# An 8192 x 8192 transpose on one core: one load issued in two parts with a meeting of the DMA engines behind it, and a branch hint in TensorE's loop

## The chip, the core and the metric

The kernel runs on one core of one Trainium2 chip. The metric is the device time of one execution in microseconds (us). Three runs of the kernel before took 1261.79, 1261.88 and 1262.31 us; their median, 1261.88 us, is the time before.

## The reference

```python
x = np.random.randn(8192, 8192).astype(np.float32)
def reference(x):
    return np.transpose(x)
```

The output is the transposed matrix in 32-bit floats. 268.44 MB are read from device memory (HBM) and 268.44 MB are written to it.

## The kernel before, in words

**Chunks.** The input is cut into T = 128 chunks of 128 rows by 4096 columns, 2 MB each (`chunks`, line 99): the left half of the columns first, from row 0 to row 8191 in 64 chunks, then the right half. Chunk t is loaded into one of NIN = 3 buffers, `ins[t % 3]`, with the 128 rows on the 128 partitions, so a load is 128 pieces of 16 KB (`load`, lines 101 to 105). The core's 16 DMA engines share each transfer: an engine takes 8 of the 128 rows. SyncE issues the first three loads; ScalarE issues all others and all stores, on its one queue, in the order of its program.

**TensorE.** `transposes(k)` (lines 112 to 123) waits until the semaphore of buffer k shows 18: 16 from the 16 DMA engines of the load, and one each from ScalarE and VectorE, which by then have emptied the PSUM halves of the chunk before. Then it makes 32 transposes of 128 x 128 blocks into the two PSUM tensors `pss[0]` and `pss[1]`. TensorE's program is a loop (lines 130 to 140) of 43 turns, three chunks in each but the first, which skips one by the `If` of line 135; the branch of line 140 closes it, and it is taken 42 times.

**Copies.** For each chunk, ScalarE copies PSUM half 0 and VectorE half 1 into the nine 2 MB regions of `regs` (line 236). A region gathers 512 output rows over W = 8 chunks; the eight groups of output rows are staggered, so that after the start one region is complete in each chunk. Before a region is filled anew, the copy waits for its earlier store (`fresh`, line 235).

**Stores and loads.** When a region is complete, `store` (lines 151 to 173) makes ScalarE wait for the copies (`s_cp`) and issue a store of 2 MB, 128 partitions by 4 output rows of up to 1024 elements. The first stores, of regions that start with fewer than eight chunks, are smaller, from 256 KB for chunk 0 up to 2 MB from chunk 7 on. At the end of chunk t's turn ScalarE waits until TensorE is done with the chunk (`s_pe`, line 250) and issues the load of chunk t + 3 (line 251). So ScalarE's program for one chunk is: copies with the store in between them or behind them, then the load of the chunk three further on. Each transfer has a semaphore that counts to 16: every DMA engine adds one, by a 4-byte packet, when its share is done. SyncE waits at the end for all stores (line 253).

Names that the prediction uses: `load`, `store`, `s_ld` (a load's semaphore), `s_st` (a store's), `regs`, and the loops of lines 133 to 140 (TensorE) and 179 to 251 (ScalarE and VectorE).

Of the kernel before, what the change touches and what calls it, by code (L numbers as in the profile page):

```python
# [24 lines left out]
def wide_dma(nc, eng, queue, out, in_):  # L25


    return eng.add_instruction(
        mybir.InstDMACopy(
            mode="Copy",  # L30
            name=nc.get_next_instruction_name(),
            engine=eng.engine,
            ins=[physical(in_)],
            outs=[physical(out)],
            queue=queue,
        )
    )
# [3 lines left out]
def kernel(  # L41
# [13 lines left out]
    nc = tc.nc  # L55
    P = 128
# [7 lines left out]
    NR = S // B  # L64
    NIN = 3
    NREG = 9
    CH = N // P
    J = S * P

    with tc.tile_critical():  # L70
        nc.alloc_sbuf_tensor("pad", [P, 32], dt)
        ident = nc.alloc_sbuf_tensor("ident", [P, P], dt).ap()
        ins = [nc.alloc_sbuf_tensor(f"in{k}", [P, J], dt).ap() for k in range(NIN)]
        SIZE = B * W * P
        regs = nc.alloc_sbuf_tensor("regs", [P, NREG * SIZE], dt).ap()
        NH = NR // 2
# [2 lines left out]
        s_id = nc.alloc_semaphore("s_id")  # L79
        s_ld = [nc.alloc_semaphore(f"s_ld{k}") for k in range(NIN)]  # L80
        s_st = [nc.alloc_semaphore(f"s_st{k}") for k in range(NREG)]
        s_pe = nc.alloc_semaphore("s_pe")
        s_cp = [nc.alloc_semaphore("s_cpa"), nc.alloc_semaphore("s_cpv")]

# [3 lines left out]
            out=ident,  # L88
            in_=ident,
# [8 lines left out]

        chunks = [(s, c) for s in range(M // J) for c in range(CH)]

        def load(t):
            s, c = chunks[t]
            (nc.sync if t < NIN else nc.scalar).dma_start(
                out=ins[t % NIN], in_=x[c * P:(c + 1) * P, s * J:(s + 1) * J]
            ).then_inc(s_ld[t % NIN], 16)

# [3 lines left out]
        def transposes(k):  # L112
            nc.tensor.sem_inc(s_ld[k], -18).wait_op(s_ld[k], 18, "sem-ge")  # L113
            for q in range(NR):
                e, g = divmod(q, NH)
                for b in range(B):
                    tr = nc.tensor.transpose(  # L117
                        pss[e][:, (g * B + b) * P:(g * B + b + 1) * P],
                        ins[k][:, q * B * P + b:(q + 1) * B * P - B + b + 1:B],
                        ident,  # L120
                    )
                if q % 2:
                    tr.then_inc(s_pe, 1)

        T = len(chunks)
# [4 lines left out]
        turn = nc.alloc_registers("turn", engines=pe)  # L130
        nc.regs_mov(turn, 0)
        nc.br("turns", engines=pe)
        with nc.body("turns", valid_engines=pe):
            now = nc.snap(turn, min_val=0, max_val=T // NIN)
            with nc.tensor.If(now > 0):
                transposes(NIN - 1)
            for k in range(NIN - 1):
                transposes(k)
            nc.regs_alu(turn, turn, 1, op=mybir.AluOpType.add)
            nc.tensor.br_lt(turn, T // NIN + 1, on_true="turns", on_false="done")  # L140
        nc.switch_bb("done")

        for t in range(NIN):
            load(t)

        copied = [0, 0]
        free = list(range(NREG))
        stored = [0] * NREG
        window = {}

        def store(q, e, count):
            t0, r, parts = window.pop(q)
            nc.scalar.wait_ge(s_cp[e], count)
            base = 0
            pieces = []
            for s, a, z in parts:
                rows = (z - a) * P
                j0 = s * J + q * B * P
                dst = out[j0:j0 + B * P, a * P:a * P + rows]
                dst = dst.rearrange("(q b) i -> q b i", q=P)  # L160
                src = regs[:, r * SIZE + base:r * SIZE + base + B * rows]
                base += B * rows
                pieces.append((rows, dst, src))
            for rows, dst, src in sorted(pieces, key=lambda v: -v[0]):
                if any(stored):
                    st = wide_dma(nc, nc.scalar, "qActDynamicHW", dst, src)
                else:
                    st = nc.scalar.dma_start(
                        out=dst, in_=src.rearrange("q (b i) -> q b i", b=B)
                    )  # L170
                st.then_inc(s_st[r], 16)
                stored[r] += 1
            free.append(r)

        def closes(w, t):
            t0, r, parts = w
            return t + 1 == t0 + sum(z - a for _, a, z in parts)

        for t, (s, c) in enumerate(chunks):
            for e in range(2):  # L180
                eng = (nc.scalar, nc.vector)[e]
                go = s_ld[(t + 1) % NIN]

                place = []
                fresh = {}
                for q in range(e * NH, (e + 1) * NH):
                    if q not in window:

                        span = (q - c) % W + 1
                        r = free.pop(0)
                        parts = [(s, c, min(c + span, CH))]
                        if c + span > CH and t + span < T:
                            parts.append((s + 1, 0, c + span - CH))
                        window[q] = (t, r, parts)
                        if stored[r]:
                            fresh[q - e * NH] = (s_st[r], 16 * stored[r])
                    t0, r, parts = window[q]
                    k = [p[0] for p in parts].index(s)  # L200
                    base = r * SIZE + B * P * sum(z - a for _, a, z in parts[:k])
                    _, a, z = parts[k]
                    place.append((base + (c - a) * P, (z - a) * P))

                runs = []
                for g in range(NH):
                    if runs:
                        u = runs[-1]
                        gap = place[g][0] - place[g - 1][0]
                        if place[g][1] == place[u[0]][1] and abs(gap) < 2 ** 15 and (  # L210
                            len(u) == 1 or gap == place[u[1]][0] - place[u[0]][0]
                        ):
                            u.append(g)
                            continue
                    runs.append([g])
                done = [g for g in range(NH) if closes(window[e * NH + g], t)]
                runs.sort(key=lambda u: any(g in fresh for g in u) - any(g in done for g in u))
                seen = t * NH + e * NH // 2
                for u in runs:
                    off, dist = place[u[0]]  # L220
                    gap = place[u[-1]][0] - place[u[-2]][0] if len(u) > 1 else 0
                    dims = [list(regs.ap[0]), [gap, len(u)], [dist, B], [1, P]]
                    o = bass.AP(regs.tensor, regs.offset + off, dims)
                    i = pss[e][:, u[0] * B * P:(u[-1] + 1) * B * P]
                    i = i.rearrange("p (l b i) -> p l b i", b=B, i=P)
                    last = u[-1]
                    if u is runs[-2:][0] and any(g in fresh for g in runs[-1]):
                        last = max(last, runs[-1][-1])
                    need = t * NH + (e * NH + last) // 2 + 1
                    if need > seen:  # L230
                        eng.wait_ge(s_pe, need)
                        seen = need
                    for g in u:
                        if g in fresh:
                            eng.wait_ge(*fresh[g])
                    cp = nc.scalar.copy(out=o, in_=i) if e == 0 else nc.vector.tensor_copy(out=o, in_=i)  # L236
                    ends = [e * NH + g for g in u if g in done]
                    if ends:
                        cp.then_inc(s_cp[e], 1)
                        copied[e] += 1  # L240
                    if u is runs[-1]:
                        if ends:
                            eng.wait_ge(s_cp[e], copied[e])
                            eng.sem_inc(go, 1)
                        else:
                            cp.then_inc(go, 1)
                    for q in ends:
                        store(q, e, copied[e])
            if t + NIN < T:
                nc.scalar.wait_ge(s_pe, (t + 1) * NR // 2)  # L250
                load(t + NIN)
        for r in range(NREG):
            nc.sync.wait_ge(s_st[r], 16 * stored[r])
# [30 lines left out]
```

## Time and profile before

| | |
|---|---|
| median of three runs | 1261.88 us |
| the profiled execution's own time | 1261.55 us |
| its span, first to last instruction | 1259.8 us |
| TensorE busy | 740.1 us, 4096 matrix instructions |
| VectorE busy | 302.6 us, 250 copies |
| ScalarE busy | 256.4 us, 256 copies |
| issues by ScalarE: loads | 125, 2048 KB each, median 22.5 us from issue to landing |
| issues by ScalarE: stores | 142; 114 of 2048 KB, median 18.4 us to landing |
| bytes moved | 536.95 MB, mean 426 GB/s |

The profile is of one execution. Its page gives the busy time of each engine, the span in 40 slices, the DMA queues (q1 is SyncE's, q10 is ScalarE's, q8 and q14 carry instructions that the engines fetch), and groups of instructions with what ended the idle time before them. The trace behind it answers for any stretch of the span: the timeline of an engine, the busy time and the DMA rate, and the number of DMA packets that start in a stretch, by size. In the loads and the 2 MB stores the only packets under 512 B are the 4-byte ones with which a DMA engine reports its share of a transfer as done. Their number in a narrow stretch therefore tells how many of the 16 engines finished a given transfer in it.

### The profile page before, as it was taken

Reading aid. Unit: us, or ns where it says so; the run is one execution under the profiler, and the core shown is the slowest. Engines: PE = TensorE matmul, PEld = TensorE weight load, DVE = VectorE, ACT = ScalarE, POOL = GpSimd, SP = SyncE. Lnnn points to the kernel's source line nnn. Section 1 sums busy time; section 2 is a strip of 40 time slices with the busy share of each in tenths; the row PEclk is TensorE's granted clock in tenths of the full one; section 3 lists DMA queues with packets and bytes.
Section 4 is the critical chain, followed back from the end, with each engine's and each line's share of the span. In section 5 each row is a group of like instructions: output and inputs, shape, how many; then the busy total and the mean of one; then the engine's idle time right before and its main releaser. Section 6 shows DMA issues by size and latency. Waiting matters only on the chain. (4 is left out here: it accounts for less than half of the span.)

```text
span 1259.8 us, 9405 instructions
## 1 busy us (share of the span) xinstructions
PE 740.1 (59%) x4096; PEld 719.5 (57%) x4096; DVE 302.6 (24%) x250; ACT 256.4 (20%) x257; POOL 0.7 (0%) x6
## 2 busy tenths in 40 slices
PE   5656656565566656565555656565566656565561
PEld 5556656565556655565555655565565656565551
DVE  2322222222222222222222222222222222222220
ACT  2212121121211211122211221221111211121120
POOL 0000000000000000000000000000000000000000
PEclk9886776768777777778687786868777786868776
DMA  9999999999999999999999999999999999999998
GB/s 385 427 427 429 429 427 431 428 430 430 428 431 428 430 432 428 430 430 429 430 424 426 431 429 429 430 429 431 429 430 431 429 430 431 428 431 429 430 431 355
DMA packets 39271, 536.95 MB, mean 426 GB/s; under 512 B 4320, under 2 KB 4832, under 8 KB 6240
## 3 DMA queue, kind: packets, MB, share of 16 engines
q10 hardware_dynamic: 38832, 530.60, 98.9%
q1 hardware_dynamic: 432, 6.29, 1.2%
q14 instruction: 6, 0.05, 0.0%
q8 instruction: 1, 0.02, 0.0%
HBM read 268.44 MB, written 268.44 MB: 426 GB/s over the span
## 5 line engine op out<-in xcount | busy, mean ns | idle before, releaser
L117 PE MATMUL ps<-ident,in 128*128 128x128 f32 x4096 | 740.1, 362 | 491.8 <-PEq L113 491.8
L117 PEld LDWEIGHTS ps<-ident,in 128*128 128x128 f32 x4096 | 719.5, 219 | 512.3 <-issue 512.3
L236 DVE COPY regs<-ps 128x512 f32<-128x512 f32 (+3 forms) x250 | 302.6, 1246 | 930.9 <-PE ps L117 903.0
L236 ACT COPY regs<-ps 128x512 f32<-128x512 f32 (+3 forms) x256 | 255.1, 1014 | 975.0 <-PE ps L117 756.7
L236 ACT ACT_TABLE_LOAD x1 | 1.3, 1283 | 1.0 <-SPq L70 1.0
L87 POOL TENSOR_SCALAR_AFFINE_SELECT ident<-ident 128x128 f32<-128x128 f32 x1 | 0.3, 294 | 0.2 <-POOL ident L85 0.2
L85 POOL MEMSET ident<- 128x128 f32 x1 | 0.2, 205 | 0.5 <-SPq L70 0.5
L268 POOL MEMSET const-bfloat16-1.0<- 128x1 bf16 x1 | 0.1, 102 | 0.0
L268 POOL MEMSET const-uint8-127<- 128x1 uint8 x1 | 0.1, 102 | 0.0
L268 POOL MEMSET const-float32-0.0<- 128x1 f32 x1 | 0.1, 99 | 0.2 <-issue 0.2
L268 POOL MEMSET const-float32-1.0<- 128x1 f32 x1 | 0.1, 99 | 0.0
## 6 DMA issues: line engine op xcount, KB each, us to landing
in<-in_x_dram ACTq DMA_DIRECT2D x125, 2048.0 KB, 22.5
out_dram<-regs ACTq DMA_DIRECT2D x114, 2048.0 KB, 18.4
out_dram<-regs ACTq DMA_DIRECT2D x4, 1792.0 KB, 15.1
in<-in_x_dram SPq DMA_DIRECT2D x3, 2048.0 KB, 11.7
out_dram<-regs ACTq DMA_DIRECT2D x4, 1536.0 KB, 15.8
out_dram<-regs ACTq DMA_DIRECT2D x4, 1280.0 KB, 15.8
out_dram<-regs ACTq DMA_DIRECT2D x4, 1024.0 KB, 17.1
out_dram<-regs ACTq DMA_DIRECT2D x4, 768.0 KB, 18.7
```

The source lines that it names most:

```text
L85: nc.gpsimd.memset(ident, 0.0).then_inc(s_id, 1)
L87: nc.gpsimd.affine_select(out=ident, in_=ident, compare_op=mybir.AluOpType.not_equal, fill=1.0, base=0, pattern=[[-1, P]], channel_multipl ...
L117: tr = nc.tensor.transpose(pss[e][:, (g * B + b) * P:(g * B + b + 1) * P], ins[k][:, q * B * P + b:(q + 1) * B * P - B + b + 1:B], ident,)
L236: cp = nc.scalar.copy(out=o, in_=i) if e == 0 else nc.vector.tensor_copy(out=o, in_=i)
L268: nc = _bacc.Bacc("TRN2", target_bir_lowering=False, num_devices=1)
```

## The change

1. The load of chunk 10 (`MEET + NIN - 1`, with `MEET = 8`) is issued as two transfers, rows 0 to 79 (`MOST = 80`, five rows for each DMA engine) and rows 80 to 127 (three rows for each). The first adds to a new semaphore, `s_most`; only the second adds to the buffer's `s_ld`.
2. In chunk 8's turn the store is not issued where its copy stands. It is held back until all copies of the turn are issued and ScalarE has seen 16 in `s_most`. The load of chunk 11 stands behind it, as before, and so do all later transfers. That load of chunk 10 is the last transfer issued ahead of the wait.
3. TensorE's loop gets one more instruction at its head in every turn, a branch prefetch hint (`mark_branch_hint_location`), tied to the branch that closes the loop.

```diff
+    MEET = 8
+    MOST = 80
...
+        s_most = nc.alloc_semaphore("s_most")
...
         def load(t):
             s, c = chunks[t]
-            (nc.sync if t < NIN else nc.scalar).dma_start(
-                out=ins[t % NIN], in_=x[c * P:(c + 1) * P, s * J:(s + 1) * J]
-            ).then_inc(s_ld[t % NIN], 16)
+            eng = nc.sync if t < NIN else nc.scalar
+            cuts = [0, MOST, P] if t == MEET + NIN - 1 else [0, P]
+            for a, z in zip(cuts, cuts[1:]):
+                eng.dma_start(
+                    out=ins[t % NIN][a:z], in_=x[c * P + a:c * P + z, s * J:(s + 1) * J]
+                ).then_inc(s_ld[t % NIN] if z == P else s_most, 16)
...
             now = nc.snap(turn, min_val=0, max_val=T // NIN)
+            hint = nc.tensor.mark_branch_hint_location()
             with nc.tensor.If(now > 0):
...
-            nc.tensor.br_lt(turn, T // NIN + 1, on_true="turns", on_false="done")
+            nc.tensor.br_lt(
+                turn, T // NIN + 1, on_true="turns", on_false="done"
+            ).branch_hint(hint)
...
+        held = []
...
                     for q in ends:
-                        store(q, e, copied[e])
+                        if t == MEET:
+                            held.append((q, e, copied[e]))
+                        else:
+                            store(q, e, copied[e])
+            if t == MEET:
+                nc.scalar.wait_ge(s_most, 16)
+                for q, e, count in held:
+                    store(q, e, count)
             if t + NIN < T:
                 nc.scalar.wait_ge(s_pe, (t + 1) * NR // 2)
                 load(t + NIN)
```

## The prediction

> **What bounds the kernel now.** I read the page first: the span in slices, then the groups with their idle time.
>
> ```profile
> span 1259.8 us, 9405 instructions
> ...
> DMA  9999999999999999999999999999999999999998
> GB/s 385 427 427 429 429 427 431 428 430 430 428 431 428 430 432 428 430 430 429 430 424 426 431 429 429 430 429 431 429 430 431 429 430 431 428 431 429 430 431 355
> ...
> L117 PE MATMUL ps<-ident,in 128*128 128x128 f32 x4096 | 740.1, 362 | 491.8 <-PEq L113 491.8
> ```
>
> The 16 DMA engines are busy throughout, at 424 to 432 GB/s in every slice but the first and the last. TensorE idles 491.8 us, always at line 113, where it waits for a load or for the copies. So the DMA engines are the bound. The question is which of the sixteen, and the windows of the trace answer it (columns: stretch and length, busy time and count of PE, PEld, DVE, ACT and POOL, then clock, DMA share, GB/s).
>
> ```profile
> 1100.00:1200.00 100.00, 61.08 (x332) 59.47 (x332) 23.86 (x20) 20.54 (x20) 0.00 (x0) 0.72 1.01 430
> ...
> 1254.20:1258.60 4.40, 0.00 (x0) 0.00 (x0) 0.00 (x0) 0.00 (x0) 0.00 (x0) 0.50 0.20 79
> ```
>
> In mid-run no engine pauses (share 1.01), and 430 / 16 = 26.9 GB/s per engine puts a 16 KB row at 0.61 us. In the last 4.4 us the share is 0.20: some engines still work while most have finished. The end is set by the engine that lags most.
>
> How large the lag is at load 10 can be counted. Three stretches, 78.9 to 80.1, 80.1 to 82.5 and 82.5 to 82.8 us; packets under 512 B are engines that report their share as done:
>
> ```profile
> DMA packets 45, 0.49 MB, mean 410 GB/s; under 512 B 15, under 2 KB 15, under 8 KB 15
> ...
> DMA packets 63, 1.03 MB, mean 430 GB/s; under 512 B 0, under 2 KB 0, under 8 KB 0
> ...
> DMA packets 8, 0.11 MB, mean 382 GB/s; under 512 B 1, under 2 KB 1, under 8 KB 1
> ```
>
> Fifteen engines finish load 10 within 1.2 us, one about 3 us later (82.6 against 79.5). The same for load 126, in 1211.85 to 1212.8, 1213.6 to 1214.2, 1214.2 to 1215 and 1215.8 to 1216.2 us (the stretches between these hold none):
>
> ```profile
> DMA packets 35, 0.39 MB, mean 414 GB/s; under 512 B 11, under 2 KB 11, under 8 KB 11
> ...
> DMA packets 17, 0.26 MB, mean 437 GB/s; under 512 B 1, under 2 KB 1, under 8 KB 1
> ...
> DMA packets 21, 0.31 MB, mean 389 GB/s; under 512 B 2, under 2 KB 2, under 8 KB 2
> ...
> DMA packets 13, 0.18 MB, mean 451 GB/s; under 512 B 2, under 2 KB 2, under 8 KB 2
> ```
>
> Eleven engines still go together, but five now lag, the last two by about 4 us behind the first. Measured from the first reporter, the late engine of load 10 went from 3.6 to 3.75 us behind to 3.95 to 4.35: it slipped 0.2 to 0.75 us in 116 chunks. The other of the last two was in the group of fifteen, so it went from at most 1.2 us to about 4.1: it slipped 2.75 us or more.
>
> **The change part by part.**
>
> *The meeting.* It removes no byte. An engine that is ahead will stand still until the late one has caught up, and that alone moves neither the late engine nor the end. Two things can move the end: whether the late engine itself runs dry, and how the sixteen slip against each other afterwards.
>
> ScalarE around the place, and TensorE's start on chunk 10 and after:
>
> ```profile
> 61.70 0.93 ACTq L103 DMA_DIRECT2D in<-in_x_dram  x1
> 65.36 0.59 ACT L236 COPY regs<-ps 128x512 f32<-128x512 f32 x1 [6.21 <-PE ps L117]
> 65.98 0.55 ACTq L28 DMA_DIRECT2D out_dram<-regs  x1
> ...
> 68.64 0.33 ACTq L103 DMA_DIRECT2D in<-in_x_dram  x1
> 77.82 1.01 ACT L236 COPY regs<-ps 128x1024 f32<-128x1024 f32 x1 [9.66 <-DMA out_dram<-regs]
> 78.86 0.55 ACTq L28 DMA_DIRECT2D out_dram<-regs  x1
> 79.45 1.01 ACT L236 COPY regs<-ps 128x1024 f32<-128x1024 f32 x1 [0.62 <-ACT regs L236]
> 79.47 0.94 ACTq L103 DMA_DIRECT2D in<-in_x_dram  x1
> ```
>
> ```profile
> 83.08 5.57 PE L117 MATMUL ps<-ident,in 128*128 128x128 f32 x32 [4.63 <-PEq L113]
> 92.80 5.57 PE L117 MATMUL ps<-ident,in 128*128 128x128 f32 x32 [4.15 <-PEq L113]
> ```
>
> Load 10 goes out at 61.70. Today store 8 (65.98) and load 11 (68.64) queue up behind it. With the change both wait for the late engine's first five rows. Its last row is reported at 82.6, so its fifth is at 82.6 - 3 x 0.61 = 80.8. From report to waiter takes 83.08 - 82.6 = 0.45 us (TensorE on chunk 10), so ScalarE issues store 8 at about 81.2. What an issue into idle engines costs, the trace shows once, at the start: SyncE issues at 0.94; the stretches are 0.94 to 1.95 and 1.95 to 2.35 us.
>
> ```profile
> 0.94 1.32 SPq L103 DMA_DIRECT2D in<-in_x_dram  x3
> ```
>
> ```profile
> DMA packets 0, 0.00 MB, mean 0 GB/s; under 512 B 0, under 2 KB 0, under 8 KB 0
> ...
> DMA packets 16, 0.26 MB, mean 655 GB/s; under 512 B 0, under 2 KB 0, under 8 KB 0
> ```
>
> That is 1.0 to 1.4 us, so data flow again at 82.2 to 82.6, just as the late engine ends its last three rows (82.6). It pauses 0 to 0.2 us; I take **+0.2**. The upper bound is ScalarE's first store, issued behind SyncE's loads: no packet of it by 14.8 us.
>
> ```profile
> 10.98 0.65 ACTq L168 DMA_DIRECT2D out_dram<-regs  x1
> ...
> q1 hardware_dynamic: 114, 1.61, 98.6%
> ```
>
> From 10.98 to 14.8 only q1 moved: 3.8 us, which would restart at 85.0 and cost 2.4 us. That store had other traffic ahead of it, so the lower row is nearer. [...]
>
> What queues behind the wait on ScalarE: store 8, load 11, then chunk 9's copies (now 77.82 and 79.45), its store and load 12. From 81.2: two issues of 0.55 and up to 0.94 us, the copy at about 82.7 to 83.7, store 9 at 83.8, the second copy to 85, load 12 by 86. Chunk 10's transposes wait for that copy: 85 instead of 83.08. TensorE's idle time covers it (4.15 us before chunk 11, whose load lands at about 92.8 in either case). Store 8 and load 11 keep the DMA engines busy, at 2.1 MB and 430 GB/s or 4.9 us each, to 82.4 + 2 x 4.9 = 92.2, and store 9 and load 12 are in the queue by then. So nothing runs dry a second time: **0**, and if store 9 came later than 92.2 its delay would be the cost.
>
> *The slip afterwards.* All sixteen start level with the late engine, so the end is now set by whichever slips most over the remaining 117 chunks. If the old slips repeat, that is the engine with about 3.2 instead of the late one with about 0.6: +2.6 (between 2.0 and 4.1 by the counts above). If the slips of the leaders came from running out of phase with the late engine, level engines would not repeat them: 0. If nothing slips at all, the late engine's own 0.6 is saved: -0.6. No row tells which. I take the middle of the first two, **+1.3**, and keep -0.6 and +2.6 for the range.
>
> *The split.* One more issue (0.33 to 0.94 us) on ScalarE at 62, hidden in the idle time before its copy at 65.36, and 16 more 4-byte packets: **0**; without that cover under 1 us once.
>
> *The hint.* One more TensorE instruction in 43 turns, beside 491.8 us of idle time: 0 on TensorE even at half a microsecond each (22 us). Its effect can only be in the fetches, which the DMA engines carry:
>
> ```profile
> q14 instruction: 6, 0.05, 0.0%
> q8 instruction: 1, 0.02, 0.0%
> ```
>
> One 16 KB packet on q8. The stretch 19 to 21 us holds it, and in it TensorE ends its first turn and branches back, at 15.48 + 4.11 = 19.6:
>
> ```profile
> q8 instruction: 1, 0.02, 2.9%
> ```
>
> ```profile
> 15.48 4.11 PE L117 MATMUL ps<-ident,in 128*128 128x128 f32 x32 [1.71 <-PEq L113]
> ```
>
> All 16 engines report load 2 in 17.3 to 17.9; fifteen report load 3 in 23.3 to 23.9 and one in 24.5 to 24.65:
>
> ```profile
> DMA packets 226, 0.11 MB, mean 179 GB/s; under 512 B 16, under 2 KB 226, under 8 KB 226
> ...
> DMA packets 52, 0.16 MB, mean 273 GB/s; under 512 B 15, under 2 KB 15, under 8 KB 51
> ...
> DMA packets 17, 0.07 MB, mean 437 GB/s; under 512 B 1, under 2 KB 1, under 8 KB 17
> ```
>
> So the fetch put about 1.0 us on one engine (0.6 to 1.35), and the late engine begins there. A hint in turn 0 runs at about 2 us, when load 0 has begun; the fetch would cost the same engine the same 1.0 under load 0. I take **0**; if it comes for free, -1.0.
>
> Sum: 1261.55 + 0.2 + 0 + 1.3 + 0 + 0 = 1263.05 us in the profiled execution's terms; the median of the runs stands 0.33 above that execution, so 1263.4.
>
> **The rivals.**
>
> *A: the engines ahead slip as before* (ends on the other side, slower). Mechanism: level engines meet the same fetches and collisions as before, and one slips 3.2 where the late one slips 0.6. Price: 0.2 + 2.6, that is 1264.7; with a pause of 2.4 it is 1266.9. It decides from a worst slip of 2.9 us on, where the sum passes 0.2%. For it: five engines did fall behind after load 10. Against: 11 of 16 didn't.
>
> *B: the hint fetches in every turn.* 42 packets of 16 KB on one engine, 0.61 to 1.0 us each: 26 to 42 us, 1288 to 1304. Against it: the kernel before takes the branch 42 times and q8 shows one packet, so the loop stays in the instruction memory. [...]
>
> *C: the fetch leaves the data's way and level engines hardly slip.* -1.0 - 0.6 + 0.2 gives 1260.5; if more of the late engine's 3.1 us at load 10 came from TensorE's fetches than the one recorded packet, another 1 to 2 us go, down to 1258.5. Against it: the one packet explains a third of the lag, and no other is recorded before load 10.
>
> *D: the meeting does not level the engines*, since restart is staggered or slips return at once: the old lag of 4 us with the pause, 1262.1.
>
> **How the numbers follow.** Forecast with D, 1261 to 1264.4: 0.43. A: 0.29. B: 0.07. C: 0.21, about half of it with further fetches. The predicted time is 1263.4. The range runs from 1259.8 (C without its far end) to 1266.9 (A with the longest pause); B and that far end of C stay out. A measurement of this kernel can tell about 0.2%, 2.5 us, from no change. Faster by more than that, below 1259.36, needs C's further fetches: 0.11. Slower by more, above 1264.4, is A and B: 0.36. Within: 0.53.
>
> **What would show it.** Store 8 issued at about 81.2 instead of 65.98; sixteen reports of load 11 within about 1 us; a dip of the DMA rate near 80 to 82.5 us only. Late in the run, reports of one load spread over 1 to 4 us: the slip. One q8 packet or none: B is wrong. My forecast is wrong if the last engine pauses over 1 us, if q8 shows tens of packets, or if the spread at the end is under 0.6 us.

## The result, and the profile after

The changed kernel takes 1269.3 us in the median of six runs (1268.34 to 1273.97), the kernel before 1262.24 us in six runs beside it (1261.79 to 1262.65). The ratio is 1.0063, with a 95% interval of 1.0047 to 1.0078: slower by 5.9 to 9.8 us. The profiled executions have spans of 1266.5 and 1259.8 us.

From the page of the changed kernel: the span, the DMA rate in 40 slices of 31.7 us, and the queues.

```profile
span 1266.5 us, 9450 instructions
...
GB/s 385 424 349 423 427 429 427 428 430 430 429 429 431 429 430 431 428 428 430 430 424 423 432 429 429 430 429 430 430 430 430 430 430 431 428 430 431 428 430 360
...
q10 hardware_dynamic: 38848, 530.60, 98.9%
q1 hardware_dynamic: 432, 6.29, 1.2%
q14 instruction: 6, 0.05, 0.0%
```

One slice stands out: 349 GB/s in the third, where the kernel before has 427. The bytes that are missing there are 78 / 429 x 31.7 = 5.8 us of full rate. And q8 has no packet in the span: the fetch at TensorE's first backward branch is gone.

Where the 6.7 us of the profiled executions arise can be read from TensorE's starts. They are the arrivals of loads 9, 10 and 11 on the last DMA engine; the kernel before has 72.92, 83.08 and 92.80.

```profile
70.86 5.56 PE L123 MATMUL ps<-ident,in 128*128 128x128 f32 x32 [3.73 <-PEq L119]
86.85 6.44 PE L123 MATMUL ps<-ident,in 128*128 128x128 f32 x32 [10.43 <-PEq L119]
96.64 6.63 PE L123 MATMUL ps<-ident,in 128*128 128x128 f32 x32 [3.35 <-PEq L119]
```

Chunk 9 starts 2.1 us earlier, chunk 10 3.8 us later. So between the two 5.8 us are lost. Chunk 11 is still 3.8 us late, the end 6.7: another 2.9 us are lost behind it. Most of them go soon: chunk 20 starts at 187.39 us instead of 181.04, 6.35 us late.

The trace also keeps the time at which each engine's report of a load lands, a little behind the start of the 4-byte packet that the windows count (below: "by the reports"). By these, the mean of the sixteen engines is 6.3 us later than before at load 10 and 6.9 at load 126. So the sixteen together lose only 0.6 us behind the meeting. The rest is one engine that falls behind the others again: the last report of load 10 lands 0.4 us behind the mean of its sixteen, that of load 20 2.8 and that of load 126 2.7.

ScalarE around the wait, and the windows of the stretch before and behind it (columns as in the prediction's windows, the last two are the DMA share and GB/s):

```profile
58.29 1.18 ACTq L109 DMA_DIRECT2D in<-in_x_dram  x2
...
81.77 0.55 ACTq L28 DMA_DIRECT2D out_dram<-regs  x1
82.35 0.60 ACTq L109 DMA_DIRECT2D in<-in_x_dram  x1
83.05 1.01 ACT L246 COPY regs<-ps 128x1024 f32<-128x1024 f32 x1 [16.35 <-issue]
```

```profile
65.00:75.00 10.00, 6.27 (x41) 6.11 (x40) 2.29 (x1) 1.44 (x1) 0.00 (x0) 0.84 1.01 424
75.00:80.00 5.00, 1.42 (x11) 1.23 (x9) 2.29 (x1) 0.00 (x0) 0.00 (x0) 0.84 1.04 239
80.00:85.00 5.00, 0.00 (x0) 0.00 (x0) 0.00 (x0) 1.33 (x2) 0.00 (x0) 0.50 1.02 157
```

Store 8 goes out at 81.77, near the 81.2 of the prediction. But no engine stands idle for it: the DMA share is 1.02 to 1.04 throughout. The rate has fallen to 239 GB/s from 75 us on, before anything waits, and to 157 GB/s in the second five microseconds. The engines are busy with the two parts of load 10, and their rows take some 1.3 us each in the mean, by the packets' own durations, where others take 0.61.

At the end the engines are apart again. Reports of one load in 1218.55 to 1219.25, 1220.5 to 1220.85, 1221.6 to 1221.7 and 1222.2 to 1222.9 us:

```profile
DMA packets 30, 0.34 MB, mean 492 GB/s; under 512 B 9, under 2 KB 9, under 8 KB 9
...
DMA packets 9, 0.10 MB, mean 281 GB/s; under 512 B 3, under 2 KB 3, under 8 KB 3
...
DMA packets 8, 0.10 MB, mean 983 GB/s; under 512 B 2, under 2 KB 2, under 8 KB 2
...
DMA packets 22, 0.33 MB, mean 468 GB/s; under 512 B 2, under 2 KB 2, under 8 KB 2
```

Nine engines go together, seven lag by 1.3 to over 3 us: as in the kernel before. At load 10 they had been level, but not by the meeting. The reports of store 7, ahead of the wait, show it: sixteen in 74.5 to 75.3 us with the change, against fifteen in 74.1 to 74.85 and one in 77.3 to 77.4 us in the kernel before.

```profile
DMA packets 36, 0.33 MB, mean 410 GB/s; under 512 B 16, under 2 KB 16, under 8 KB 16
```

```profile
DMA packets 35, 0.33 MB, mean 437 GB/s; under 512 B 15, under 2 KB 15, under 8 KB 15
...
DMA packets 4, 0.05 MB, mean 492 GB/s; under 512 B 1, under 2 KB 1, under 8 KB 1
```

The late engine is gone before the wait, and with the hint alone (next section) it is gone too. So it is the hint that levels the engines in the changed kernel.

### The profile page after: what moved, and what is told of

It reads as the page before. It is cut to its first block, busy times and chain, and to the rows that moved or that the text cites. A ratio compares the mean times of both kernels' runs of the same rounds, so it can differ in the third digit from the quotient of the medians.

```text
span 1266.5 us, 9450 instructions
## 1 busy us (share of the span) xinstructions
PE 740.2 (58%) x4096; PEld 719.6 (57%) x4096; DVE 302.6 (24%) x250; ACT 256.4 (20%) x257; POOL 0.7 (0%) x6
```

## The experiments

Each run's kernel was timed beside the kernel before; the differences below are to those runs. All are given in the median.

**One part of the change at a time.** First the hint alone: the diff of TensorE's loop is kept, the rest undone.

```diff
+            hint = nc.tensor.mark_branch_hint_location()
...
-            nc.tensor.br_lt(turn, T // NIN + 1, on_true="turns", on_false="done")
+            nc.tensor.br_lt(
+                turn, T // NIN + 1, on_true="turns", on_false="done"
+            ).branch_hint(hint)
```

> The hint alone: load 10 whole, no wait. In the changed kernel the last DMA engine reported store 7 at 76.0 us instead of 77.7, so the hint seems to take one or two instruction fetches (1 us each) off one engine early on. Theory S (slips come back whatever the start): the last engine is about 1.7 us earlier at 80 us, but other engines fall behind later and the spread at the end is again about 4 us: 1261.5 to 1262.3. Theory F (the others only slip because of the late engine): the spread at the end stays under 1.5 us and the time is 1259 to 1260. Theory H (the hint costs time): over 1262.5, with packets on q8 in every turn.

1263.07 us against 1261.61; ratio 1.0015 (1.0006 to 1.0024). Theory H's range, over 1262.5, has the number, but not for its reason: q8 has no packet in the span. Chunk 9 starts 2.1 us early, as in the changed kernel, so what the hint removes is real. It is lost again. A part goes in the window 83 to 132 us, first with the hint alone, then in the kernel before.

```profile
70.83 6.46 PE L120 MATMUL ps<-ident,in 128*128 128x128 f32 x32 [3.69 <-PEq L116]
```

```profile
83.00:132.00 49.00, 30.77 (x152) 29.96 (x151) 11.67 (x7) 10.12 (x10) 0.00 (x0) 0.67 1.01 424
```

```profile
83.00:132.00 49.00, 29.58 (x160) 28.77 (x160) 11.59 (x7) 10.13 (x10) 0.00 (x0) 0.71 1.01 429
```

With no late engine all sixteen together are slower, 424 instead of 429 GB/s, which is 0.6 us in this window. By the reports, the last engine is 2.3 us early at load 10 and 1.6 us late at load 126: in between the sixteen lose 2.7 us in the mean, and the last one falls 1.3 us further behind the mean.

Then the split alone: 80 and 48 rows, no wait, no hint.

```diff
+            cuts = [0, MOST, P] if t == MEET + NIN - 1 else [0, P]
+            for a, z in zip(cuts, cuts[1:]):
+                eng.dma_start(
+                    out=ins[t % NIN][a:z], in_=x[c * P + a:c * P + z, s * J:(s + 1) * J]
+                ).then_inc(s_ld[t % NIN] if z == P else s_most, 16)
```

> Load 10 in two parts of 80 and 48 rows, no wait and no hint. [...] Theory W (the wait is what costs): 1261.9 to 1262.3, no dip.

1269.26 us, 7.6 more, without the wait, and so far above theory W's range: 5.0 us are there at chunk 10 and 7.0 at the end of the profiled execution. The slice and the start of chunk 10 show the same loss as the changed kernel (348 GB/s in the third slice; 88.08 instead of 83.08):

```profile
GB/s 386 425 348 427 427 429 429 429 430 429 430 430 430 428 429 430 429 429 430 429 420 425 429 430 430 429 430 430 430 428 430 430 430 430 429 430 430 429 430 350
```

```profile
88.08 5.21 PE L123 MATMUL ps<-ident,in 128*128 128x128 f32 x32 [9.72 <-PEq L119]
```

So the loss in the slice belongs to the split, not to the wait.

**The wait without the dear split.** Load 10 is cut by columns, so both parts have all 128 rows.

```diff
-    MOST = 80
+    MOST = 2560
...
-            cuts = [0, MOST, P] if t == MEET + NIN - 1 else [0, P]
+            cuts = [0, MOST, J] if t == MEET + NIN - 1 else [0, J]
...
-                    out=ins[t % NIN][a:z], in_=x[c * P + a:c * P + z, s * J:(s + 1) * J]
+                    out=ins[t % NIN][:, a:z], in_=x[c * P:(c + 1) * P, s * J + a:s * J + z]
```

> The changed kernel, but load 10 is cut by columns: 2560 columns of all 128 rows first, then 1536 columns. Bytes per engine, wait and hint are the same as in the changed kernel; only the rows' fall on the partitions is that of a whole load. [...] Theory W: 1267 to 1269, as in the changed kernel.

> As the run with columns and the wait, but without the hint: this is the case of the prediction's sum (meeting of unequal engines, no dear split). [...] Theory F (level engines slip little): 1261.3 to 1262.2. Theory W: 1267 or more.

With the hint 1265.88 us, 4.3 more than before; without it 1267.94, 6.3 more. The dear split is gone, and still the run without the hint lies in theory W's range, and the one with it only 1.1 us below. So the wait itself costs far more than I had put down. In the run without the hint, ScalarE's issue, TensorE's start on chunk 11, and then the rate in slices:

```profile
80.65 0.55 ACTq L28 DMA_DIRECT2D out_dram<-regs  x1
```

```profile
94.18 5.57 PE L123 MATMUL ps<-ident,in 128*128 128x128 f32 x32 [3.74 <-PEq L119]
```

```profile
GB/s 384 426 375 422 421 425 425 426 430 428 431 430 431 429 430 430 428 430 430 429 421 423 429 430 430 430 430 431 429 429 429 430 430 429 430 431 430 430 429 359
```

Chunk 11 starts 1.4 us late (94.18 against 92.80), the end is 6.1 us late (span 1265.9): 4.7 us come after the meeting is long over. In the slices from 95 to 250 us the rate is 421 to 426 GB/s, where the kernel before has 427 to 431.

The first 1.4 us are no pause of the last engine. Its last report of load 10 falls at 82.12. Of the sixteen engines' first rows of store 8, fifteen start in the stretch 81.8 to 82.1 us, and the sixteenth starts in 82.1 to 82.15 us, together with that report:

```profile
DMA packets 16, 0.25 MB, mean 840 GB/s; under 512 B 0, under 2 KB 0, under 8 KB 1
...
DMA packets 2, 0.02 MB, mean 328 GB/s; under 512 B 1, under 2 KB 1, under 8 KB 1
```

What follows is slow although the engines are busy, 324 GB/s at a share of 1.02:

```profile
84.00:88.00 4.00, 3.28 (x16) 3.31 (x17) 0.00 (x0) 0.58 (x1) 0.00 (x0) 0.50 1.02 324
```

By the packets' own durations, the last rows of store 8, and then those of load 11, take up to about 1.2 us instead of 0.61. The run with the hint has the same: its engines are level ahead of the wait, none stands for more than 0.6 us between load 10 and store 8, and still the sixteen lose 2.1 us in the mean between loads 10 and 11, by the reports. So a part of the wait's cost lies in the two transfers behind it, and why they are slow is open. Of the 4.7 us further on, in the run without the hint, the sixteen lose 2.3 in the mean; the rest is one engine that falls behind anew, from 0.3 us behind the mean at load 11 to 2.8 at load 126.

Next the cover is made longer: 1024 columns first, 3072 behind them, so that each engine still has 3.7 us of work when the last one reports.

```diff
-    MOST = 2560
+    MOST = 1024
```

> The wait at chunk 8 with load 10 cut by columns, no hint, but 1024 columns first and 3072 behind them, so that each engine still has 3.7 us of work when the last one reports (before: 1.8 us, and 1267.9 us in the median). If the pause of the last engine, about 1.0 us, was part of the cost, it goes: 1266.5 to 1267.2. If the whole cost is the slipping behind the wait: 1267.6 to 1268.3.

1265.47 us, 3.5 us more than the kernel before, against 6.3 with 2560 columns: the gain is larger than either expectation had it. The reports of store 8 now spread over 85.76 to 87.11 us instead of 87.42 to 88.04: with a longer cover the engines ahead wait less and are levelled only in part. There was no pause to save. The run fits that levelling costs, but it doesn't show it: the wait also ends at another moment of the load.

**Why the split is dear.** Four loads cut into 80 and 48 rows; load 10 in halves; load 10 in 32, 64 and 32 rows. No wait, no hint.

```diff
-            cuts = [0, MOST, P] if t == MEET + NIN - 1 else [0, P]
+            cuts = [0, MOST, P] if t in (10, 40, 70, 100) else [0, P]
```

```diff
+            cuts = [0, 64, P] if t == MEET + NIN - 1 else [0, P]
```

```diff
+            cuts = [0, 32, 96, P] if t == MEET + NIN - 1 else [0, P]
```

> Loads 10, 40, 70 and 100 each in parts of 80 and 48 rows, no wait, no hint. One such split alone cost 7.6 us in the median (5.0 of them by the end of load 10). Theory P (each split load takes two loads' time): 4 x 5 = 20 us and some slips, 1281 to 1290, with four dips of the rate. A rival by which the split disturbs only the start (queue order, phases): 1267 to 1271.

> Load 10 in rows 0 to 63 and 64 to 127, no wait, no hint. [...] Rival (few rows for each engine are dear by themselves, or an odd row count is): four rows for each engine in both halves, so plus 0 to 1, 1261.5 to 1263.

> Load 10 in rows 0 to 31, 32 to 95 and 96 to 127, no wait, no hint. [...] Rival (more parts, more cost): three parts cost more than two, over 1267.

Four splits: 1282.84 us, 20.8 more, 5.2 for each, with four dips (349, 364, 358, 366) in the page's rate:

```profile
GB/s 384 428 349 425 422 431 427 428 430 430 430 364 423 430 429 431 429 431 429 429 422 358 430 428 431 429 431 429 431 429 366 430 430 430 430 429 431 429 430 363
```

Halves: 1266.92, 4.9 more. Quarter, half, quarter: 1265.30, 3.3 more (ratio 1.0023, 1.0014 to 1.0033), though it has one part more. The profiled execution of the three parts took 1271.01 us, 5.7 above the median; by the reports it is 3.5 us late at load 10, and the rest of its loss comes behind load 56, so its windows at 75 to 83 us can be read. The windows of the halves:

```profile
75.50:77.50 2.00, 2.00 (x14) 2.00 (x13) 0.00 (x0) 0.00 (x0) 0.00 (x0) 0.65 0.95 205
78.00:80.00 2.00, 0.38 (x4) 0.19 (x2) 1.58 (x1) 1.33 (x2) 0.00 (x0) 1.00 0.94 213
80.50:82.50 2.00, 0.00 (x0) 0.00 (x0) 0.21 (x1) 0.03 (x1) 0.00 (x0) 0.50 1.01 205
```

and of the three parts:

```profile
75.50:77.50 2.00, 2.00 (x11) 2.00 (x10) 0.00 (x0) 0.00 (x0) 0.00 (x0) 0.50 0.85 205
78.00:80.00 2.00, 1.30 (x10) 1.10 (x9) 0.67 (x1) 1.38 (x2) 0.00 (x0) 0.96 1.05 352
80.50:82.50 2.00, 0.00 (x0) 0.00 (x0) 1.12 (x1) 0.12 (x1) 0.00 (x0) 0.77 1.00 246
```

The halves run at 205 to 213 GB/s, half of 430. Rows 0 to 31, a quarter of the load, run at 205 too, and the middle 64 rows come to 352 in a window that still has the late engine's quarter in it. So it is not the number of rows or parts that decides: 64 rows move at 205 in one place and come to 352 in another, and what differs is the partitions they fall on. Why some partitions together are slow, no run shows. For the change's two parts, 1.31 MB and 0.79 MB, an estimate: if each needs the 4.9 us of a whole load (2.1 MB at 430 GB/s), that is 267 and 160 GB/s, and the changed kernel shows 239 and 157. The 4-byte packets of the first part start at 79.7 to 80.7 us and those of the second at 84.6 to 86.0, some 5 us apart.

**Why the wait is dear.** The wait with columns at chunk 30, when the engines have long settled, and the same with copies that move 8 of each 128 columns from chunk 24 on.

```diff
-    MEET = 8
+    MEET = 30
```

```diff
+                    if t >= 24:
+                        dims[-1] = [1, 8]
+                        o = bass.AP(regs.tensor, regs.offset + off, dims)
+                        i = i[:, :, :, 0:8]
```

> The wait with load 32 cut by columns (chunk 30 instead of chunk 8), no hint; by then the engines of the kernel before have settled at lags up to 3.8 us. Theory S (level engines collide and slip apart anew, whenever they are levelled): as with the wait at chunk 8, plus 4 to 6.5: 1265.5 to 1268, rate down to 421 to 426 for some 150 us behind the wait, lags at the end again 4 to 5 us. Rival E (the slips belong to the first 200 us of the program): only the pause of about 1.0 to 1.5 us, 1262.5 to 1263.5, lags at the end under 1.5 us.

> The wait at chunk 30 with columns, no hint; from chunk 24 on the copies out of PSUM move only 8 of each 128 columns, so most of the output isn't the transpose. Loads, stores and waits are all there. Theory X (the copies' writes into SBUF stretch the rows that level engines load at the same time): level engines keep the pace of 9.77 us for each chunk, and the time is 1262.5 to 1264. Rival Y (the cause lies among the DMA engines or in device memory, not in the copies): level engines again take about 9.98 us for each chunk and slip by 4 to 5 us: 1266.5 to 1268.5.

1268.01 us (6.0 more) and 1268.71 us (6.7 more). So slips don't belong to the start of the program: levelled at 300 us, the engines slip apart anew, and with a sixteenth of the copies' writes the cost is no smaller. The window 303.5 to 400 us in the kernel before, with the wait at chunk 30, and with small copies besides:

```profile
303.50:400.00 96.50, 56.71 (x310) 55.09 (x310) 23.65 (x17) 18.19 (x15) 0.00 (x0) 0.76 1.01 429
```

```profile
303.50:400.00 96.50, 56.45 (x309) 54.84 (x308) 23.55 (x17) 18.95 (x14) 0.00 (x0) 0.75 1.00 421
```

```profile
303.50:400.00 96.50, 53.88 (x288) 52.43 (x288) 3.64 (x17) 3.02 (x13) 0.00 (x0) 0.73 1.00 414
```

429, 421 and 414 GB/s. With VectorE and ScalarE busy 3.6 and 3.0 us instead of 23.6 and 19.0, level engines are no faster. These windows begin with load 33, which is the second of the two slow transfers behind the wait. From 310 us on, in the same order:

```profile
310.00:400.00 90.00, 54.43 (x298) 52.97 (x297) 21.36 (x16) 17.98 (x14) 0.00 (x0) 0.75 1.01 429
```

```profile
310.00:400.00 90.00, 54.02 (x294) 52.57 (x295) 21.26 (x16) 17.42 (x13) 0.00 (x0) 0.75 1.01 426
```

```profile
310.00:400.00 90.00, 53.88 (x288) 52.43 (x288) 3.35 (x16) 3.02 (x13) 0.00 (x0) 0.73 1.01 421
```

So level engines lose 3 GB/s of 429 where nothing waits. By the reports, the pace follows the spread: with the wait at chunk 30 the sixteen reports of a load stay within 0.5 to 1.3 us of each other from load 33 to 46, and a load takes 9.86 us; from load 56 to 66 they lie 3.6 to 4.0 us apart, and a load takes 9.77 us, as in the kernel before. How level they are shows in the reports of one load, all sixteen in 338.5 to 339.1 us (wait at chunk 30):

```profile
DMA packets 32, 0.26 MB, mean 437 GB/s; under 512 B 16, under 2 KB 16, under 8 KB 16
```

From 310 to 400 us the rows that take clearly longer than 0.61 us are, by the packets' own durations, nearly all among the last four of a load, in the 2.6 us ahead of its reports and so ahead of the store that follows.

**Is one late engine a help?** The hint alone, and one more small transfer that a single DMA engine has to carry.

```diff
+        nc.sync.dma_start(out=pad[0:P - 1], in_=x[0:P - 1, 0:32]).then_inc(s_pad, 16)
```

> The hint alone, and behind SyncE's three loads one more transfer, 127 rows of 128 bytes, which one DMA engine has to carry by itself: it is late by some 2 us from 20 us on, as the late engine of the kernel before was by the fetches. Theory L (level engines stretch each other's rows; one late engine early on helps the others apart, which is why the hint alone didn't pay): as the kernel before, 1261.5 to 1262.3. Rival (the hint's own loss of 1.5 us has another cause, and a late engine only adds): 1263 to 1265.

1261.88 us against 1261.98; ratio 1.0003 (0.9995 to 1.0012). The page has 560 packets on q1 instead of 432: the 127 rows and a single 4-byte report, where a load has sixteen, so one engine carried them all. It is late more slowly than expected: by the reports the last is 0.3 us behind the mean at load 3 and 2.2 at load 8. No loss of the hint is measured, and 83 to 132 us shows nearly the rate of before:

```profile
83.00:132.00 49.00, 29.50 (x160) 28.66 (x159) 11.58 (x7) 10.12 (x10) 0.00 (x0) 0.77 1.01 428
```

Each against the kernel before timed beside it, one late engine turns the hint's 1.5 us into -0.1. The two intervals just overlap (1.0006 to 1.0024 for the hint alone), so the size of this is uncertain. What theory L asks for is there: by the reports, from load 10 to load 126 the sixteen lose 0.1 us in the mean with the late engine and 2.7 with the hint alone.

**Do the issues stretch the rows?** Two spare copies on ScalarE ahead of each store's issue from chunk 24 on, with the wait at chunk 30 and, as a control, without any wait.

```diff
+            if t >= 24:
+                rep = bass.AP(ident.tensor, ident.offset, [list(ident.ap[0]), [0, 16], [1, P]])
+                for _ in range(2):
+                    nc.scalar.wait_ge(s_id, 2 + len(spent))
+                    spent.append(nc.scalar.copy(out=junk.rearrange("p (r i) -> p r i", i=P), in_=rep).then_inc(s_id, 1))
```

> The wait at chunk 30 with columns, no hint; from chunk 24 on ScalarE makes two copies of 1.9 us into a spare buffer ahead of each store's issue, so store and load are issued some 3.7 us later in the chunk. In the run without them (1268.0) the stretched rows were the last ones of each load, 0 to 2 us behind the issues. Theory I (the issue of new transfers stretches the rows that are under way): the stretched rows move out of the loads' end into the stores, or vanish; if they vanish, level engines keep 9.77 us for each chunk and the time is 1262.5 to 1265. Rival T (the turn from load to store of all engines at one time is what stretches): still the last rows of the loads, 9.9 to 10 us for each chunk, 1266.5 to 1269.

> Control: the kernel before with the same two spare copies ahead of each store's issue from chunk 24 on, no wait, load 10 whole, no hint. ScalarE idles over 6 us in a chunk, and a load is issued 22 us ahead of its landing, so 3.7 us later costs nothing: 1261.5 to 1262.5. If issues that fall into the loads of settled engines cost too (theory I), 1263 to 1266.

1273.24 and 1266.89 us: both slower, the control too, by 4.7. The control loses it at the very end, where the last stores come late for queues that have run dry: by the reports its last load lands 0.5 us later than in the kernel before, and its span is 3.9 us longer. Its windows:

```profile
1180.00:1220.00 40.00, 24.78 (x136) 24.14 (x135) 9.67 (x9) 24.29 (x25) 0.00 (x0) 0.76 1.01 430
1240.00:1262.00 22.00, 0.00 (x0) 0.00 (x0) 0.00 (x0) 20.47 (x12) 0.00 (x0) 0.50 0.69 291
```

The control was badly chosen for that, and both expectations missed. Against it, the wait costs 6.35 us, and 6.0 without the spare copies. But the issues moved less than the 3.7 us planned: between 310 and 400 us the stores go out 1.9 to 4.3 us later than without the spare copies, and the loads' reports themselves come 1.2 to 1.5 us later. The long rows stay at the loads' ends, though there are fewer. That speaks against the issues as the cause, but doesn't exclude them. That the turn of all engines from load to store is the cause is left over, not shown.

No version beat the kernel before; the hint with one late engine equals it.

## Why the prediction was wrong, point by point

**The split, put at 0: the step that failed.** The prediction counted one more issue and 16 small packets and took it for granted that 80 and 48 rows move at the rate of 128. The runs show 5.8 us between chunks 9 and 10 in the changed kernel, 7.6 us in the median for the split alone, 5.2 for each of four. Each part takes as long as a whole load, some 5 us. The row that could have warned was missing: no transfer of the kernel before is cut by rows, and the prediction gave this term no upper bound beside the issue's 1 us.

**The slip behind the wait, +1.3 within -0.6 to 2.6.** In the changed kernel it was 2.9 us, near rival A's 2.6: engines that start level slip apart again. But the prediction had the wait level them, and it was the hint. With the wait alone (columns, no hint) 4.7 us come behind the meeting, and 2.5 of them are this slip. The other 2.3 stood in no term, nor did the 1.4 of the two slow transfers behind the wait. The working looked only at how far engines fall behind the first. It missed that level engines lose together: 421 to 426 instead of 427 to 431 GB/s from 95 to 250 us, where nothing waits. The reason given for a slip of 0, that leaders only slip because of a late engine, was the wrong way round: the hint alone costs 1.5 us, and with one engine late no cost is measured.

**The pause, +0.2.** This term was right. In the changed kernel no pause came, because the dear second part still ran when store 8 was issued. With a cheap split and no hint, the last engine went from load 10 to store 8 without a gap. ScalarE issued store 8 0.39 us after the last report of the first part (80.26 to 80.65), near the 0.45 that the prediction read from TensorE's start. That store 8 went out near the forecast in the changed kernel (81.2 against 81.77) is luck in part: the last engine was 2.1 us early by the hint, and its first part took 5 us instead of 3. What queues behind it on ScalarE was as forecast.

**The hint, 0 or -1.0.** The fetch is gone from the span, and more than it: chunk 9 starts 2.1 us earlier. In the kernel before, the last engine is 1.0 us behind the mean at load 3 and 2.7 at load 9, with no second fetch recorded in between; with the change it is 0.4 at load 9. So the lag that begins with the fetch grows without another. Rival B is out: q8 has no packet in the span. Rival C's gain doesn't reach the end, because of the slip: alone the hint costs 1.5 us. Where the wait levels the engines in any case it saves 2.1 (1265.88 against 1267.94).

**The end is set by the last engine:** right, but only half of what bounds the kernel. In medians, each against the kernel before timed beside it, the runs make the sum: hint alone +1.5, the wait with it by columns +4.3, by rows +7.1. The last step, 2.8, is less than the split costs alone. By the reports, between loads 10 and 11 the sixteen lose 2.1 us with columns and none with rows. So the slow second part seems to take the place of the slow transfers behind the wait; no run tests this.

## What to carry to other kernels

Cut by columns where it can be had: with the wait and the hint, the third slice of the page has 396 GB/s when load 10 is cut by columns and 349 when it is cut by rows. Price any transfer of fewer than 128 partitions by a row of the trace; here a part's rate went with the partitions that its rows fell on, 205 to 213 GB/s for halves of 64 rows and 352 in the window of the middle 64. Letting queues meet removes no work from the slowest one, and engines that run level may be slower than engines that have drifted apart (426 against 429 GB/s here): look at the rate of the whole group in the stretch behind, not only at who is last. A saving early in a bandwidth-bound kernel is not a saving at its end until the end shows it.

## What the runs showed of the hardware that was not expected

- Parts of a load on fewer partitions moved more slowly: 205 to 213 GB/s for halves of 64 rows, 205 for 32 rows on partitions 0 to 31, and 352 for 64 rows on partitions 32 to 95 with the late engine's quarter besides, against 430 for 128 rows.
- Sixteen level DMA engines that alternate loads and stores of 2 MB moved 426 GB/s from 310 to 400 us, the same engines spread over 3.8 us 429. Levelled at 80 or at 300 us, they end 4.4 and 4.9 us apart again. The cause is open.
- ScalarE's store, issued at 80.65 us when most DMA engines were idle (columns, no hint), had its first packets on the way about 1.2 us later, at 81.86, near the 1.0 to 1.4 us of SyncE's first load.
